# Light and heavy experts of a mixture taking turns step by step, with value products of attention on column tiles

## The chip, the cores and the metric

The kernel runs on one core of a Trainium2 chip. The core has a matrix engine (TensorE), a vector engine (VectorE), a scalar engine (ScalarE), GpSimd, and SyncE, which here issues the DMA transfers in program order ("SP" in the profile). Products are accumulated in eight PSUM banks of 128 partitions by 512 fp32 values. The metric is the time of one execution on the device in microseconds, the median of the runs.

## The reference, cut to what matters

The program is a stack of layers on 256 rows of 1024 values: retention, a feed-forward layer, dilated attention, a feed-forward layer, a layer that joins a convolution mixer and neighborhood attention, a feed-forward layer, a Fourier mixer, and a mixture of experts. All is fp32. The two attentions and the mixture are what the change touches:

```python
p = softmax(scores + bias)                    # per head and block of 128 queries
o = einsum('bhqk,bhkd->bhqd', p, v)           # head width 64 (dilated) or 32 (neighborhood)

logits = h @ w_router + b_router              # 8 experts
top_val, top_idx = lax.top_k(logits, 2)       # each row goes to 2 of them
out = zeros_like(h)
for e in range(8):
    out = out + gate[..., e:e+1] * ((silu(h @ w1[e]) * (h @ w3[e])) @ w2[e])   # 1024 -> 3584 -> 1024
```

## The kernel before, in words

**Mixture of experts.** The router's choices are counted per expert, and `order_experts` ranks the experts by their number of rows on VectorE (expert 0 is always rank 0; the count of the other ranks decides). Ranks 0 to 3 are "heavy" and handled on a tile of 128 rows, ranks 4 to 7 are "light" and handled on 64 rows. If an expert has more rows than its tile, a second pass at the end does the rest; it is skipped here at run time.

For each expert, `select` writes a 0/1 matrix P (Pz for a light one) from the row positions `posm`, and `gather` multiplies it with the rows: the expert's own rows, transposed, come out (`hgh`, `hgl` for a heavy one, `hx` for a light one). Then come seven steps `u`, each over 512 of the 3584 hidden columns. A step has two parts:

- `first` loads 512 columns of `w1` and of `w3`, 2 MB each, into wide slots (`rawx` and `rawy`, a ring of four), and multiplies. A heavy expert splits each fp32 weight into a high and a low part (`wh` by ScalarE at L113, `wl` by VectorE at L114) and does three products for each (L1067), on the whole 128x128 array. A light one takes the fp32 weights as they are, with 64 columns of rows standing, so that `w1` goes to the upper and `w3` to the lower column tile of the array in turn (L1055). ScalarE and VectorE then form silu times product (`tm`, L1163 and L1164).
- `turn` transposes this by TensorE (L1078) into `eTh`, `eTl` or `eTx`, and `back` multiplies it with two 1 MB units of `w2` (ring of `raw` and `x`), on the whole array (L1107) or on column tiles (L1095). In the program this second part of a step is written after the first products of the next step.

At step 6 `spread` transposes P, and `scatter` adds the result, weighted by the gate, to the rows (L1135, L1136). The plan runs one whole expert after another: heavy rank 0 with all its seven steps, light rank 4 with its seven, heavy rank 1, and so on. Loads are issued by SyncE in the order in which the program uses them, each when its slot is free. PSUM has four banks for products (`mm`), two for transposes (`tp`) and two for the rest (`aux`).

**Attention.** For one head and one block of 128 queries, the scores S are products in an `aux` bank. `attend` adds the bias with a running minimum (L388, VectorE), takes the exponential (L390, ScalarE), normalizes (L392, L393, VectorE), transposes by TensorE (L396) and copies to P (L398, ScalarE). Then four value products follow (L488 in the dilated attention, 64 columns wide; L932 in the neighborhood attention, 32 wide), each on the columns of the array that the head's number gives. The heads are written one after another.

The functions that the change touches:

Of the kernel before, what the change touches and what calls it, by code (L numbers as in the profile page):

```python
# [18 lines left out]
F32 = mybir.dt.float32  # L19
# [33 lines left out]
class Net:  # L53
    def __init__(s, tc, a, out, ctx):
# [10 lines left out]
        s.ps = s.pool("psum", 1, space=PSUM)  # L65
# [10 lines left out]

    def mm_tile(s, shape, name="mm"):
        return s.ps.tile(shape, F32, name=name, tag="mm", bufs=4)

    def tp_tile(s, shape, name="tp"):  # L80
        return s.ps.tile(shape, F32, name=name, tag="tp", bufs=2)

    def aux_tile(s, shape, name="aux"):
        return s.ps.tile(shape, F32, name=name, tag="aux", bufs=2)
# [296 lines left out]
    def attend(s, pool, S, bias):  # L381
# [15 lines left out]
        P = pool.tile([128, 4, 128], F32, name="P")  # L397
# [3 lines left out]
    def dilated(s, x, xt):  # L401
        nc = s.nc
        with ExitStack() as ctx:
# [24 lines left out]
            for qd in range(4):  # L428
# [47 lines left out]
                for h in range(4):  # L476
                    c, e = h // 2, h % 2
                    hs = slice(64 * h, 64 * h + 64)
                    for b in range(2):
                        order = [(0, 0), (1, 0), (2, 0), (0, 1)] if b == 0 else [(0, 0), (0, 1), (1, 1), (2, 1)]  # L480
                        S = s.aux_tile([128, 4, 128])
                        for n, (g, kb) in enumerate(order):
                            nc.tensor.matmul(out=S[:, n, :], lhsT=Q[g][:, c, e, b * 128:b * 128 + 128],
                                             rhs=K[g][:, c, kb * 128:kb * 128 + 128], start=True, stop=True)
                        P = s.attend(p, S.rearrange("p n c -> p (n c)"),
                                     bias[:, h, 1 - b:5 - b, :].rearrange("p n c -> p (n c)"))
                        for n, (g, kb) in enumerate(order):
                            nc.tensor.matmul(out=O[64 * e:64 * e + 64, c, b * 128:b * 128 + 128],  # L488
                                             lhsT=V[g][:, kb, hs], rhs=P[:, n, :], start=n == 0, stop=n == 3)
# [416 lines left out]
    def neighborhood(s, ctx, yt):  # L906
# [4 lines left out]
        for c in range(4):  # L911
            O = s.mm_tile([128, 256])
            for hh in range(4):
                h = 4 * c + hh
                bt = biases[h % 2]
                for r2 in range(2):
                    src = bass.AP(tensor=rpb.tensor, offset=rpb.offset + h * 1905 + (5 - r2) * 127,
                                  ap=[[1, 64], [127, 6], [1, 64]])
                    nc.sync.dma_start(out=bt[64 - 64 * r2:128 - 64 * r2, 4:10, :], in_=src)
                nc.vector.tensor_tensor(out=bt[:, 4:10, :], in0=bt[:, 4:10, :],  # L920
                                        in1=mask[:, None, :].to_broadcast([128, 6, 64]), op=ALU.add)
                ds = slice(32 * h, 32 * h + 32)
                for b in range(2):
                    S = s.aux_tile([128, 2, 256])
                    q = qps[c // 2][:, c % 2, hh, b * 128:b * 128 + 128]
                    nc.tensor.matmul(out=S[:, b, :], lhsT=q, rhs=kt[:, c, :], start=True, stop=True)
                    nc.tensor.matmul(out=S[:, 1 - b, :], lhsT=q, rhs=s.kc[:, c, :], start=True, stop=True)
                    P = s.attend(p, S.rearrange("p n c -> p (n c)"),
                                 (bt[:, 6:14, :] if b == 0 else bt[:, 0:8, :]).rearrange("p m c -> p (m c)"))
# [74 lines left out]
    def experts(s, pc, m, plan, ss):  # L1004
# [136 lines left out]
        def prepare(n):  # L1141
            r, light, base = plan[n]
            P = select(r, light, base)
            return P, gather(P, light)

        ready, last = prepare(0), None
        for n, (r, light, _) in enumerate(plan):
            P, x = ready
            for u in range(7):
                g = first(r, light, u, x)  # L1150
                pms = next(g)
                hid = turn(last[1], last[3]) if last else None
                if pms is None:
                    pms = next(g)
                if n + 1 < len(plan) and u == (3 if plan[n + 1][1] != light else 6):
                    ready = prepare(n + 1)
                if last:
                    s.second(back, spread, scatter, last, hid, None)
                if u == 0:
                    po = [s.mm_tile([128, 512]) for _ in range(1 if light else 2)]  # L1160
                rows = 64 if light else 128
                sg = s.np.tile([128, 512], F32, name="tm")
                nc.scalar.activation(out=sg[0:rows], in_=pms[0], func=AF.Silu)  # L1163
                nc.vector.tensor_tensor(out=sg[0:rows], in0=sg[0:rows], in1=pms[1], op=ALU.mult)  # L1164
                last = r, light, u, sg, po, P
# [34 lines left out]
    def order_experts(s, q, pk, m, pc, posm, gate, iota, tri8):  # L1200
# [3 lines left out]
        cn = q.tile([128, NE], F32, name="cn")  # L1204
        nc.vector.tensor_copy(cn, pc)
# [25 lines left out]
        ids = pk.tile([128, NE], I32, name="ids")  # L1231
        by_rank(idf, iota[:, 0:NE])
        nc.vector.tensor_scalar(out=ids, in0=idf, scalar1=-1.0, scalar2=None, op0=ALU.add)
        m.posm = pk.tile([128, 2, NE], F32, name="posr")
        m.gate = pk.tile([128, 2, NE], F32, name="gater")
        for t in range(2):
            by_rank(m.posm[:, t, :], posm[:, t, :])
            by_rank(m.gate[:, t, :], gate[:, t, :])
# [5 lines left out]
        cnt = pk.tile([128, 1], I32, name="cnt")  # L1244
        nc.vector.tensor_copy(cnt, cf)
        return ids, cnt

    def moe(s, x):
# [5 lines left out]
        with ExitStack() as ctx:  # L1254
# [15 lines left out]
            with ExitStack() as c2:  # L1270
# [50 lines left out]
                for t in range(2):  # L1321
# [12 lines left out]
                ids, cnt = s.order_experts(q, pk, m, pc, posm, gate, iota, tri8)  # L1334
            ss = pk.tile([128, 2, 2], F32, name="ss")
            _, regs = nc.values_load_multi_w_load_instructions(ids[0:1, 1:NE], engines=(mybir.EngineType.SP,),
                                                               min_val=0, max_val=NE - 1)
            m.ids = [0] + list(regs)
            heavy, light = list(range(NH)), list(range(NH, NE))
            plan = []  # L1340
            for i in range(max(len(heavy), len(light))):
                plan += [(r, False, 0) for r in heavy[i:i + 1]] + [(r, True, 0) for r in light[i:i + 1]]
            with ExitStack() as c2:
                s.experts(s.pool("moe_c", 1, c2), m, plan, ss)
# [245 lines left out]
```

## Time and profile before

| | us |
|---|---|
| median of three runs | 2341.37 (2340.36 to 2343.44) |
| the profiled execution | 2343.06 |
| its span, first to last instruction | 2341.2 |
| TensorE busy | 2244.8 (96% of the span) |
| VectorE busy | 1482.3 (63%) |
| ScalarE busy | 1079.1 (46%) |
| DMA, 639.74 MB | mean 273 GB/s |

The span is cut into instructions per engine, each with its start, its duration, its line of the kernel and the tiles it writes and reads (out<-in). Idle time before an instruction is put down to what ended it. A fp32 matmul can leave more than one record, and the recorded end of a matmul lies after the start of the next, since they are pipelined; so the distance of starts is the rate. TensorE's granted clock is given for a stretch as a share of full speed; its mean over the span is 0.980.

### The profile page before, as it was taken

How to read it: one execution, taken by the hardware profiler on the slowest of the kernel's cores; microseconds unless marked ns; L12 is line 12 of the kernel's file. 1: busy time of each engine (PE TensorE's matmuls, PEld its weight loads, DVE VectorE, ACT ScalarE, POOL GpSimd, SP SyncE). 2: the span in 40 equal slices, each digit the busy share in tenths (PEclk: the TensorE clock that was granted, in tenths of full speed). 3: DMA queues.
4: the chain of work that ended last, by engine and by line, in shares of the span. 5: the costliest groups of instructions: out<-in, count | busy, mean ns of one | idle time of the engine just before them, and what ended most of it. 6: DMA issues, size and time to landing. Idle time of an engine off the chain costs nothing. (4 is left out here: it accounts for less than half of the span.)

```text
span 2341.2 us, 34240 instructions
## 1 busy us (share of the span) xinstructions
PE 2244.8 (96%) x13729; PEld 1792.7 (77%) x13729; DVE 1482.3 (63%) x2018; ACT 1079.1 (46%) x1424; POOL 33.4 (1%) x39
## 2 busy tenths in 40 slices
PE   8999999999999999999899997999999999999996
PEld 8987988899998998987799786863685378447832
DVE  6987897867746555785665557850794179228821
ACT  4433543454444544655544445740673167126611
POOL 0000000000000000100000000000000000000000
PEclk9999999999999999999999997999999999999998
DMA  8676778777642554642365636889998999899986
GB/s 316 240 257 220 279 258 287 263 261 264 238 167 105 203 195 168 222 157 41 112 212 205 240 116 259 338 326 426 424 406 329 412 425 392 331 426 425 391 345 250
DMA packets 99710, 639.74 MB, mean 273 GB/s; under 512 B 22551, under 2 KB 33432, under 8 KB 39512
## 3 DMA queue, kind: packets, MB, share of 16 engines
q1 hardware_dynamic: 99128, 636.71, 71.1%
q8 instruction: 109, 1.79, 0.3%
q10 hardware_dynamic: 416, 0.78, 0.1%
q14 instruction: 57, 0.47, 0.1%
HBM read 634.17 MB, written 3.28 MB: 272 GB/s over the span
## 5 line engine op out<-in xcount | busy, mean ns | idle before, releaser
L113 ACT ACTIVATE wh<-raw 128x1024 fp32r<-128x1024 f32 x476 | 502.6, 1060 | 569.2 <-PE mm L154 263.2
L114 DVE TENSOR_TENSOR wl<-raw,wh 128x1024 fp32r<-128x1024 f32 x476 | 576.2, 1221 | 250.4 <-ACT wh L113 247.6
L154 PE MATMUL mm<-xTh,wh 128*128 128x256 f32 x1600 | 447.4, 280 | 0.7 <-ACT tm L816 0.7
L154 PE MATMUL mm<-xTh,wl 128*128 128x256 f32 x1600 | 446.0, 279 | 0.0
L154 PE MATMUL mm<-xTl,wh 128*128 128x256 f32 x1600 | 445.3, 278 | 0.0
L154 PEld LDWEIGHTS mm<-xTh,wh 128*128 128x128 f32 x1600 | 301.2, 188 | 7.5 <-issue 5.6
L154 PEld LDWEIGHTS mm<-xTh,wl 128*128 128x128 f32 x1600 | 300.8, 188 | 4.1 <-issue 4.1
L154 PEld LDWEIGHTS mm<-xTl,wh 128*128 128x128 f32 x1600 | 301.1, 188 | 3.5 <-issue 3.5
L1164 DVE TENSOR_TENSOR tm<-tm,mm 128x512 f32<-128x512 f32 (+1 forms) x56 | 38.0, 679 | 252.8 <-ACT tm L1163 252.8
L1067 PE MATMUL mm<-wh,hgh 128*128 128x512 f32 x448 | 179.9, 402 | 0.0
L1067 PE MATMUL mm<-wl,hgh 128*128 128x512 f32 x448 | 178.8, 399 | 0.0
L1067 PE MATMUL mm<-wh,hgl 128*128 128x512 f32 x448 | 177.5, 396 | 0.0
L170 PE MATMUL mm<-wh,xTh 128*128 128x256 f32 x608 | 173.8, 287 | 2.9 <-ACT wh L113 2.5
L170 PE MATMUL mm<-wh,xTl 128*128 128x256 f32 x608 | 174.1, 287 | 1.5 <-DVE xTl L144 1.5
L170 PE MATMUL mm<-wl,xTh 128*128 128x256 f32 x608 | 173.8, 286 | 0.6 <-DVE wl L114 0.5
L114 DVE TENSOR_TENSOR wl<-rawx,wh 128x1024 fp32r<-128x1024 f32 x128 | 150.7, 1220 | 16.1 <-ACT wh L113 15.0
L113 ACT ACTIVATE wh<-rawx 128x1024 fp32r<-128x1024 f32 x128 | 133.0, 1059 | 38.4 <-PE mm L1067 14.7
L1055 PE MATMUL mm<-rawy,hx 128*64 128x512 f32 x512 | 135.4, 637 | 14.2 <-DMA rawy<-in_moe_w_dram 14.2
L526 DVE CUSTOM_DVE_ANT_0 araw<-araw,cond 128x1024 f32<-128x1024 f32 x96 | 115.7, 1217 | 27.0 <-DMA araw<-in_w_ada_dram 26.9
L1163 ACT ACTIVATE tm<-mm 128x512 f32<-128x512 f32 (+1 forms) x56 | 33.0, 589 | 206.3 <-PE mm L1055 199.0
L170 PEld LDWEIGHTS mm<-wh,xTh 128*128 128x128 f32 x608 | 117.8, 194 | 5.3 <-ACT wh L113 2.9
L170 PEld LDWEIGHTS mm<-wh,xTl 128*128 128x128 f32 x608 | 118.5, 195 | 2.8 <-DVE xTl L144 2.3
(358 smaller groups left out, 3670.2 us busy)
## 6 DMA issues: line engine op xcount, KB each, us to landing
rawx<-in_moe_w_dram SPq DMA_DIRECT2D x56, 2048.0 KB, 9.7
rawy<-in_moe_w_dram SPq DMA_DIRECT2D x56, 2048.0 KB, 11.9
raw<-in_moe_w_dram SPq DMA_DIRECT2D x84, 1024.0 KB, 14.7
araw<-in_w_ada_dram SPq DMA_DIRECT2D x48, 1024.0 KB, 5.1
raw<-in_ffn_w_up_dram SPq DMA_DIRECT2D x44, 1024.0 KB, 4.8
raw<-in_attn_w_in_dram SPq DMA_DIRECT2D x36, 1024.0 KB, 5.0
raw<-in_ffn_w_dram SPq DMA_DIRECT2D x33, 1024.0 KB, 4.9
x<-in_moe_w_dram SPq DMA_DIRECT2D x28, 1024.0 KB, 12.2
```

The lines of the kernel that those rows point to most:

```text
L113: nc.scalar.activation(out=h, in_=v, func=AF.Copy)
L114: nc.vector.tensor_tensor(out=l, in0=v, in1=h.bitcast(F32), op=ALU.subtract)
L154: s.nc.tensor.matmul(out=p[:, j, :], lhsT=a[:, kc, :], rhs=b[:, kc, :], start=n == 0, stop=n == 23)
L170: s.nc.tensor.matmul(out=p[:, tb if to is None else to, :], lhsT=a[:, kc, tb, :], rhs=b[:, kc % 4, :], start=n == 0, stop=n == 23)
L526: nc.vector.tensor_tensor_reduce(out=out, in0=r[:, j, :], in1=cond[src], scale=1.0, scalar=0.0, op0=ALU.mult, op1=ALU.add, accum_out=dst)
L1055: nc.tensor.matmul(out=ps[half], lhsT=x[:, kc, :], rhs=w[:, kc, :], start=kc == 0, stop=kc == 7)
L1067: nc.tensor.matmul(out=pm, lhsT=a[:, kc, :], rhs=b[:, kc % 2, :], start=n == 0, stop=n == 23)
L1163: nc.scalar.activation(out=sg[0:rows], in_=pms[0], func=AF.Silu)
L1164: nc.vector.tensor_tensor(out=sg[0:rows], in0=sg[0:rows], in1=pms[1], op=ALU.mult)
```

## The change

- The plan is a list of single steps. It begins with two steps of the first heavy expert and then takes a light and a heavy step in turn, so that the four light experts (28 steps) run beside the four heavy ones (28 steps).
- While the experts run, PSUM has five banks for products, one for transposes and two for the rest.
- The ranking of the experts is written behind the first step of the first expert, whose rows are gathered ahead of it (rank 0 needs no ranking). The positions, gates and counts that this needs are copied to tiles of their own.
- In both attentions two heads go through the scores and `attend` together, and their value products are written in turn, one for each head, so that neighbours stand on different column tiles. P has four buffers.

The core of the diff:

```diff
+            s.banks(5, 1, 2)
...
-            heavy, light = list(range(NH)), list(range(NH, NE))
-            plan = []
-            for i in range(max(len(heavy), len(light))):
-                plan += [(r, False, 0) for r in heavy[i:i + 1]] + [(r, True, 0) for r in light[i:i + 1]]
+            heavy = [(r, False, 0, u) for r in range(NH) for u in range(7)]
+            light = [(r, True, 0, u) for r in range(NH, NE) for u in range(7)]
+
+            plan = heavy[:2]
+            for i in range(max(len(heavy) - 2, len(light))):
+                plan += light[i:i + 1] + heavy[i + 2:i + 3]
...
-        ready, last = prepare(0), None
-        for n, (r, light, _) in enumerate(plan):
-            P, x = ready
-            for u in range(7):
-                g = first(r, light, u, x)
+        ready, last, late = {}, None, None
+        prepare(*order[False].pop(0))
+        for n, (r, light, _, u) in enumerate(plan):
+            P, x, po = ready[r]
+            g = first(r, light, u, x)
+            pms = next(g)
+            hid = turn(last[1], last[3]) if last else None
+            if pms is None:
                 pms = next(g)
...
+            if n == 1 and rank:
+                rank()
+                if order[True]:
+                    late = True
+            if late is not None and order[late]:
+                prepare(*order[late].pop(0))
+            late = None
+            if u == 6 and order[light]:
+                if n + 1 < len(plan) and plan[n + 1][1] == light:
+                    prepare(*order[light].pop(0))
+                else:
+                    late = light
+            if last:
+                s.second(back, spread, scatter, last, hid, None)
...
                 for b in range(2):
...
+                    P = []
+                    for hh, bt in enumerate(biases, h0):
+                        S = s.aux_tile([128, 2, 256])
...
+                        P.append(s.attend(p, S.rearrange("p n c -> p (n c)"),
+                                          (bt[:, 6:14, :] if b == 0 else bt[:, 0:8, :]).rearrange("p m c -> p (m c)")))
                     vs = [vt, vt, s.vc, s.vc] if b == 0 else [s.vc, s.vc, vt, vt]
                     for n in range(4):
-                        nc.tensor.matmul(out=O[32 * hh:32 * hh + 32, b * 128:b * 128 + 128],
-                                         lhsT=vs[n][:, n % 2, ds], rhs=P[:, n, :], start=n == 0, stop=n == 3,
-                                         tile_position=(0, 32 * hh))
+                        for i, hh in enumerate((h0, h0 + 1)):
+                            nc.tensor.matmul(out=O[32 * hh:32 * hh + 32, b * 128:b * 128 + 128],
+                                             lhsT=vs[n][:, n % 2, 128 * c + 32 * hh:128 * c + 32 * hh + 32],
+                                             rhs=P[i][:, n, :], start=n == 0, stop=n == 3, tile_position=(0, 32 * hh))
```

TensorE, in the middle of a light expert before. L1055 are the first products, L1095 those with `w2`, L1078 the turns:

```order
L1095 MATMUL mm<-raw,eTx 64x512 x8
L1078 MATMUL tp<-ident,tm 128x64 x4
L1055 MATMUL mm<-rawx,hx 64x512 x16
L1095 MATMUL mm<-raw,eTx 64x512 x4
L1095 MATMUL mm<-x,eTx 64x512 x4
L1055 MATMUL mm<-rawy,hx 64x512
```

TensorE in the change, in the middle of the stage, where L1079 is the last product with `w3` of a heavy step, L1107 the light expert's `w2`, L1090 the heavy step's turn, L1067 the first products of the next light step and L1119 the heavy expert's `w2`:

```order
L1079 MATMUL mm<-wl,hgh 128x512
L1107 MATMUL mm<-raw,eTx 64x512 x8
L1090 MATMUL tp<-ident,tm 128x128 x4
L1067 MATMUL mm<-rawx,hx 64x512 x16
L1119 MATMUL mm<-wh,eTh 128x512 x2
L1119 MATMUL mm<-wh,eTl 128x512 x2
L1119 MATMUL mm<-wl,eTh 128x512 x2
```

The products of a light step, which stood in one row with those of the next light step, now stand in two groups of 8 and 16 among the heavy step's products on the whole array, and the light step's own turn stands between the heavy products too.

VectorE ahead of the first gather before: `hm` are the modulated rows, `mrl` their low part, `byr` the ranking's work tile, P the first selection matrix:

```order
L1284 TENSOR_TENSOR hm<-hm,brow 128x512
L1227 TENSOR_TENSOR byr<-iota,R 128x64
L1228 TENSOR_REDUCE idf<-byr 128x8
L1233 TENSOR_SCALAR ids<-idf 128x8
...
L1243 TENSOR_REDUCE cf<-cr 128x1
L1245 CAST cnt<-cf 128x1
L1023 TENSOR_SCALAR P<-iota,posr 128x128 x2
```

The same place on VectorE in the change:

```order
L1340 SCALAR_TENSOR_TENSOR posm<-aux,sel 128x16
L1365 COPY cn<-aux 128x8
L1363 COPY posr<-posm 128x2
L150 TENSOR_TENSOR mrl<-hm,mrh 128x512
L1035 TENSOR_SCALAR P<-iota,posr 128x128 x2
L1229 COPY key<-cn 128x8
```

P now stands ahead of the ranking, which begins with `key`.

## Rows read from the trace of the kernel before

**Rows 1.** 25 us windows: TensorE, weight loads, VectorE, ScalarE, GpSimd busy; granted clock; DMA share, GB/s.

```profile
1705.00:1730.00 25.00, 25.00 (x111) 20.30 (x111) 22.24 (x21) 20.32 (x23) 0.00 (x0) 1.00 1.01 422
...
1755.00:1780.00 25.00, 25.00 (x113) 16.90 (x113) 16.82 (x18) 13.89 (x16) 0.00 (x0) 1.00 0.72 285
...
1830.00:1855.00 25.00, 24.16 (x112) 8.33 (x109) 1.36 (x2) 2.26 (x5) 0.00 (x0) 1.00 1.02 429
...
1855.00:1880.00 25.00, 21.95 (x89) 11.46 (x90) 10.38 (x11) 9.84 (x13) 0.00 (x0) 0.86 1.01 426
...
1405.00:1430.00 25.00, 10.88 (x49) 10.53 (x49) 15.90 (x60) 4.36 (x8) 0.26 (x1) 0.50 0.61 243
```

**Rows 2.** TensorE's waits from 1400 us on: releaser, total us, times, longest.

```profile
PE mm L1055 <- DMA rawy<-in_moe_w_dram: 14.2, 5, 3.5
...
PE mm L1055 <- DMA rawx<-in_moe_w_dram: 4.6, 2, 3.4
```

**Rows 3.** TensorE's timeline, two turns in heavy steps: start, duration, instruction.

```profile
1721.08 0.60 PE L1078 MATMUL tp<-ident,tm 128*128 128x128 f32 x4
...
1738.26 0.60 PE L1078 MATMUL tp<-ident,tm 128*128 128x128 f32 x4
```

**Rows 4.** TensorE's timeline in a light expert: an undisturbed step, then one that waits.

```profile
1804.54 1.07 PE L1055 MATMUL mm<-rawy,hx 128*64 128x512 f32 x2
...
1805.54 0.44 PE L1036 MATMUL aux<-P,mrh 128*128 128x128 f32 x2
...
1808.69 6.65 PE L1055 MATMUL mm<-rawy,hx 128*64 128x512 f32 x29
...
1819.14 0.46 PE L1078 MATMUL tp<-ident,tm 64*128 64x64 f32 x4
...
1819.53 1.94 PE L1055 MATMUL mm<-rawx,hx 128*64 128x512 f32 x8
...
1854.14 0.46 PE L1078 MATMUL tp<-ident,tm 64*128 64x64 f32 x4
...
1858.05 9.25 PE L1055 MATMUL mm<-rawy,hx 128*64 128x512 f32 x29 [3.45 <-DMA rawy<-in_moe_w_dram]
...
1871.09 0.46 PE L1078 MATMUL tp<-ident,tm 64*128 64x64 f32 x4
```

**Rows 5.** The page's DMA issues of expert weights: count, size, us to landing.

```profile
rawx<-in_moe_w_dram SPq DMA_DIRECT2D x56, 2048.0 KB, 9.7
...
rawy<-in_moe_w_dram SPq DMA_DIRECT2D x56, 2048.0 KB, 11.9
...
raw<-in_moe_w_dram SPq DMA_DIRECT2D x84, 1024.0 KB, 14.7
...
x<-in_moe_w_dram SPq DMA_DIRECT2D x28, 1024.0 KB, 12.2
```

**Rows 6.** SyncE's DMA queue, first wide loads of two heavy experts.

```profile
1648.74 5.40 SPq L104 DMA_DIRECT2D rawx<-in_moe_w_dram  x2
...
1873.99 5.40 SPq L104 DMA_DIRECT2D rawx<-in_moe_w_dram  x2
```

**Rows 7.** VectorE's timeline ahead of the first selection matrix.

```profile
1413.13 1.89 DVE L1284 TENSOR_TENSOR hm<-hm,brow 128x512 f32<-128x512 f32 x3
...
1417.34 0.22 DVE L1227 TENSOR_TENSOR byr<-iota,R 128x64 f32<-128x64 f32 x1
...
1421.61 0.48 DVE L1023 TENSOR_SCALAR P<-iota,posr 128x128 fp32r<-128x128 f32 x2
```

**Rows 8.** The same window view, of the neighborhood attention.

```profile
1046.00:1131.00 85.00, 82.33 (x533) 63.18 (x532) 50.38 (x151) 46.37 (x103) 0.00 (x0) 1.00 0.22 50
```

**Rows 9.** Groups of instructions in that stage: busy us, mean ns, idle before.

```profile
L932 PE MATMUL mm<-P,vc 128*32 128x128 f32 x128 | 19.4, 275 | 0.3 <-ACT P L398 0.3
...
L398 ACT ACTIVATE P<-tp 128x512 f32<-128x512 f32 x32 | 18.6, 593 | 22.2 <-PE tp L396 22.2
```

**Rows 10.** TensorE's timeline there, four records of value products.

```profile
1072.32 0.62 PE L932 MATMUL mm<-P,nv 128*32 128x128 f32 x4 [0.31 <-ACT P L398]
```

More of the change, by code (lines that the diff above doesn't have):

```diff
@@ L64, in __init__ @@
         s.dp = s.pool("scratch", 1, space=DRAM)
[L65 removed]
+        s.psx = ctx.enter_context(ExitStack())
+        s.banks(4, 2, 2)
         s.ident = s.con.tile([128, 128], F32, name="ident")
@@ new lines, in neighborhood @@
+            for h0 in range(0, 4, 2):
+                for hh, bt in enumerate(biases, h0):
+                    for r2 in range(2):
+                        src = bass.AP(tensor=rpb.tensor, offset=rpb.offset + (4 * c + hh) * 1905 + (5 - r2) * 127,
+                                      ap=[[1, 64], [127, 6], [1, 64]])
+                        nc.sync.dma_start(out=bt[64 - 64 * r2:128 - 64 * r2, 4:10, :], in_=src)
+                    nc.vector.tensor_tensor(out=bt[:, 4:10, :], in0=bt[:, 4:10, :],
+                                            in1=mask[:, None, :].to_broadcast([128, 6, 64]), op=ALU.add)
+                for b in range(2):
+                    P = []
+                    for hh, bt in enumerate(biases, h0):
+                        S = s.aux_tile([128, 2, 256])
+                        q = qps[c // 2][:, c % 2, hh, b * 128:b * 128 + 128]
+                        nc.tensor.matmul(out=S[:, b, :], lhsT=q, rhs=kt[:, c, :], start=True, stop=True)
+                        nc.tensor.matmul(out=S[:, 1 - b, :], lhsT=q, rhs=s.kc[:, c, :], start=True, stop=True)
+                        P.append(s.attend(p, S.rearrange("p n c -> p (n c)"),
+                                          (bt[:, 6:14, :] if b == 0 else bt[:, 0:8, :]).rearrange("p m c -> p (m c)")))
@@ L1002, in fourier, with experts @@
             return s.gated_residual(x, po, grow, then)
-    def experts(s, pc, m, plan, ss):
+    def experts(s, pc, m, plan, ss, rank=None):
         nc = s.nc
@@ L1139, in scatter, with prepare @@
                         s.squares(m.acc[:, t, :], c, ss[:, t, :], s.tp_tile([128, 512]))
-        def prepare(n):
-            r, light, base = plan[n]
+        def prepare(r, light, base):
             P = select(r, light, base)
-            return P, gather(P, light)
-        ready, last = prepare(0), None
-        for n, (r, light, _) in enumerate(plan):
-            P, x = ready
-            for u in range(7):
-                g = first(r, light, u, x)
-                pms = next(g)
[L1152 to L1165, printed above, removed]
@@ new lines, in prepare @@
+            ready[r] = P, gather(P, light), []
+        order = {k: [x[:3] for x in plan if x[1] == k and x[3] == 0] for k in (False, True)}
+        ready, last, late = {}, None, None
[6 more added lines that the diff above has]
+            if pms is None:
+                pms = next(g)
+            if n == 1 and rank:
[12 more added lines that the diff above has]
+                s.second(back, spread, scatter, last, hid, None)
+            if u == 0:
+                po.extend(s.mm_tile([128, 512]) for _ in range(1 if light else 2))
+            rows = 64 if light else 128
+            sg = s.np.tile([128, 512], F32, name="tm")
+            nc.scalar.activation(out=sg[0:rows], in_=pms[0], func=AF.Silu)
+            nc.vector.tensor_tensor(out=sg[0:rows], in0=sg[0:rows], in1=pms[1], op=ALU.mult)
+            last = r, light, u, sg, po, P
@@ L1230, in order_experts @@
         idf = q.tile([128, NE], F32, name="idf")
-        ids = pk.tile([128, NE], I32, name="ids")
         by_rank(idf, iota[:, 0:NE])
-        nc.vector.tensor_scalar(out=ids, in0=idf, scalar1=-1.0, scalar2=None, op0=ALU.add)
-        m.posm = pk.tile([128, 2, NE], F32, name="posr")
-        m.gate = pk.tile([128, 2, NE], F32, name="gater")
+        nc.vector.tensor_scalar(out=m.idt, in0=idf, scalar1=-1.0, scalar2=None, op0=ALU.add)
+        _, regs = nc.values_load_multi_w_load_instructions(m.idt[0:1, 1:NE], engines=(mybir.EngineType.SP,), min_val=0,
+                                                           max_val=NE - 1)
+        m.ids += list(regs)
         for t in range(2):
-            by_rank(m.posm[:, t, :], posm[:, t, :])
-            by_rank(m.gate[:, t, :], gate[:, t, :])
+            for out, v in ((m.posm, posm), (m.gate, gate)):
+                r = q.tile([128, NE], F32, name="byr1")
+                by_rank(r, v[:, t, :])
+                nc.vector.tensor_copy(out[:, t, 1:NE], r[:, 1:NE])
         cr = q.tile([128, NE], F32, name="cr")
```

79 lines of the change are left out of this document (35 added, 44 removed).

## The prediction

> **What bounds the kernel now.** I read the chain of waits of TensorE over the expert stage first, then 25 us windows of one pair of experts, then the issues of the weight loads, then TensorE's own timeline inside one step of each kind.
>
> The expert stage takes 40% of the time (it starts near 1400 us of 2341.2), and TensorE is nearly always busy there. But it is busy with different limits. While a heavy expert runs, TensorE, VectorE (22.2 of 25 us) and the DMA engines (share 1.01) are all full [rows 1]. The row at the end of the heavy expert shows the DMA share fall to 0.72 and the rate to 285 GB/s: the slots are full, and TensorE sets the pace. While the light expert runs, VectorE does 1.4 of 25 us, and the DMA share climbs back to 1.02 at 429 GB/s; in the next window TensorE's granted clock is 0.86 [rows 1]. So the light half drains the weight buffers and at its end waits for a transfer. The waits say the same: TensorE waited 14.2 us for `rawy` and 4.6 us for `rawx`, 18.8 us in all [rows 2].
>
> Two periods give the sizes. One heavy step lasts 1738.26 - 1721.08 = 17.2 us between two turns [rows 3]. One undisturbed light step takes 1819.14 - 1808.69 = 10.45 us plus the 0.39 us to the next step's first matmul, so 10.84 us; the step whose load came late takes 1871.09 - 1854.14 = 16.95 us, with a wait of 3.45 us inside it [rows 4]. Of the 6.1 us too much, 3.45 are the wait and the other 2.66 follow it: 29 matmuls take 9.25 us behind the wait where they took 6.65, and the granted clock is lower there. Each microsecond waited costs 6.11 / 3.45 = 1.77 us.
>
> Demand against supply: the loads of the eight experts are 56 + 56 of 2 MB and 84 + 28 of 1 MB [rows 5], 336 MB (binary), 352.3 million bytes, 88.1 for one heavy and one light expert. At 426 GB/s that is 206.8 us. The first wide load of a heavy expert is issued at 1648.74 and of the next at 1873.99, so a pair takes 225.3 us [rows 6]. There are 18.5 us per pair, 74 in four, between the pace of today and the pace of the DMA alone. That is the most that any order of the steps could give.
>
> **Part by part: taking turns.** The steps stay the same, so TensorE's work stays, 17.2 + 10.84 = 28.0 us for one heavy and one light step. The loads of two such steps are 12.58 million bytes, 29.5 us at 426 GB/s. Inside a stretch of plain steps the DMA would thus fall behind by 1.5 us per two steps, 10 us in seven; gathers and scatters, in which nothing is consumed, give it back (225.3 minus all 8.3 us of wait and lowered clock, which I work out next, is 217, and 217 is more than 206.8). A transfer lands 9.7 to 14.7 us after its issue in this stage [rows 5], so the slots hold about that backlog. I therefore let nearly all waits for weights go: 18.8 us times 1.77 is 33.3 us, or 8.3 per pair. I leave 2 us of them in. Bounds: nothing gained (the waits only move), and 74 us (DMA alone is the limit).
>
> **More changes between whole array and column tiles.** In the order before, light steps stand in a row and TensorE stays on its two column tiles, except for the turns. In the order of the change, one light step's second half and the next one's first half are two separate islands among full-array matmuls, and the 64-row turn stands between full-array matmuls too: one more island per light step, 27 in all. What an island costs has rows on both sides. Leaving the tiles for a turn and coming back shows nothing: turn at 1819.14, tiles again at 1819.53, which is what four transposes take [rows 4]. A lone pair of tile matmuls between gather matmuls takes 1805.54 - 1804.54 = 1.00 us, where a pair in a stream takes 0.43 (28 spacings of 29 matmuls in 6.65 - 0.59 us, 0.216 each): 0.57 too much [rows 4]. I take the middle, 0.28 us, because the islands are 8 and 16 matmuls long and only their edges are bare: 27 x 0.28 = 7.7 us lost; bounds 0 and 15.4.
>
> **Ranking behind the first gather.** TensorE stands idle until the first selection matrix P is there, at a granted clock of 0.50 in that window [rows 1]. VectorE writes P at 1421.61; from 1417.34 on it has done small ranking operations, and a single large one of 0.69 us [rows 7]. 4.27 - 0.69 = 3.6 us go, and another 0.9 us of ranking that stood ahead of the modulation at 1413.13 (some ten small operations, partly beside waits). I count 4.5 us; bounds 3 and 6. The register load of the expert numbers now stands in SP's queue ahead of the second expert's loads, but the slots are full at this time (243 GB/s in the window) [rows 1], so nothing is lost there. The ranking itself now lies on VectorE beside the first heavy step's splits, some 4 us late for one step, while its loads wait for free slots anyway.
>
> **Five product banks, one for turns.** Two experts in flight need three banks for their sums, and two are left for products, as before in a heavy expert. One bank for turns makes a turn wait for the copy of the one before; turns are 10 us apart, so I count nothing, and 0.5 us at the tail, where four squares share the bank. It would cost more only if spread and turn of two experts fell together, about 1 us at each of eight ends.
>
> **Attention.** The neighborhood stage is 85 us with TensorE busy 82.3, VectorE 50.4 and ScalarE 46.4 [rows 8]. Its value products are 32 columns wide and one after another. A set of scores (one head, one block of queries) has four, and the trace two records for each, 256 for the 32 sets, half of them in the row shown [rows 9]. Four records take 0.62 us, and one 0.275, so they follow each other by 0.115 us [rows 9, 10] and a set takes 0.92. On two column tiles in turn two heads should run at once, as the halves of a light expert do, so half of that, 0.46 us per set and 14.7 us in all, is the most. The dilated stage has as many sets (4 groups of heads, 4 heads, 2 blocks), on 64 columns: 14.7 us again by the same spacing. Against this stands the chain of a set: ScalarE already waits 22.2 us for the transposed scores [rows 9], and both heads of a pair must now be ready before the first product. Bounds 0 and 29.4; I take 11, somewhat under the middle, since TensorE is the fullest of the three by far.
>
> **The sum.** -33.3 + 2 + 7.7 - 4.5 + 0.5 - 11 = -38.6 us. The profiled execution took 2343.06 us (1.7 above the median of the runs, 2341.37), so 2304.5 in its terms and 2302.8 in the median's. I say 2303.
>
> **Rivals.** (a) Islands cost a drain at either edge. A tile matmul lasts 0.59 us and the stream moves by 0.216, so emptying the array costs up to 0.37 us, twice per island: 27 x 0.75 = 20 us in place of 7.7, and 2315. For it: the lone pair. Against it: the turn at 1819.14. The Trainium skill has it as a rule ("TensorEngine Tiling (Array Packing)", section "Key Properties"): a change of tiling mode, not of the tile alone, drains TensorE. The rows here agree for the lone pair and not for the turn. Chance 0.15. (b) The attention chain is bound by its latency, and pairs gain nothing: 2314. For it ScalarE's 22.2 us, against it TensorE's 82.3 of 85. Chance 0.12. (c) The DMA is the bound all through: the backlog of 1.5 us per two steps grows past what the slots hold and half of the wait comes back, 17 us: 2320. Chance 0.07. (d) Slower: in the mixed order, the light step's silu product queues on VectorE and ScalarE behind the splits of a heavy weight that has not landed, and TensorE waits for both. It decides from the point at which a pair of steps loses 38.6 / 27 = 1.4 us more; at 2 us it is 2357. For it: the engines work strictly in order and a split waits for its transfer. Against it: they would be loaded 16 of 28 us where it is now 22.2 of 25. Chance 0.07. (e) The turn-taking does nothing since loads wait in one SP queue in the same order as they are used, and starved steps only move: about 2330 with attention and start. Chance 0.05. The forecast has 0.54.
>
> **Range and chances.** (a), (b) and (c) lie inside 2280 to 2325; the low end is attention at its full 29.4 (18 less) with islands nearly free (4 to 5 less). Outside are (d), most of (e) and a little of the rest at either end. A difference under 0.2% (4.7 us) can hardly be told from none here. Faster: the forecast, (a) to (c) and (e) but for a few hundredths, 0.90. Same 0.03, slower 0.07.
>
> **What would show it.** Right: TensorE's waits for `rawx` and `rawy` under 3 us in all; no window of the stage under clock 0.95; a period of 215 to 219 us for 14 steps; DMA share nearly even over the stage, 0.93 to 1.0; the first gather at 1417; the neighborhood stage 6 us shorter. Wrong: gaps of 0.3 us or more at each end of the column-tile matmuls (a); ScalarE waits in attention as long as the saving (b); rows of DMA waits spread over heavy and light matmuls (c); waits of TensorE for `tm`, `wh` or `wl` (d). The forecast fails altogether if the slots are handed out in an order in which a light load that is not needed yet holds the place of a heavy one that is.

## The result, and the profile after

| | before | changed |
|---|---|---|
| median of four runs, us | 2342.4 (2340.36 to 2344.18) | 2315.03 (2311.44 to 2317.26) |
| profiled execution, us | 2343.06 | 2317.26 |
| its span, us | 2341.2 | 2315.2 |

The changed kernel is faster: the ratio to the kernel before is 0.9883, with a 95% interval from 0.9871 to 0.9895, so 27.4 us by the medians. The prediction was 2303, 38.6 us less than the 2341.37 it started from.

The waits of TensorE from 1380 us to the end, in the changed kernel (engine, tile and line that waited, what ended the wait, total, times, longest):

```profile
PE aux L1338 <- DVE sel L1336: 7.0, 1, 7.0
PE mm L1079 <- DVE wl L120: 4.1, 3, 1.4
PE aux L1147 <- ACT n L149: 4.0, 5, 1.5
```

No wait for `rawx` or `rawy` is left; there were 18.8 us of them [rows 2]. The windows of 25 us (columns as in [rows 1]) show what took their place:

```profile
1765.00:1790.00 25.00, 25.00 (x113) 16.00 (x111) 15.93 (x15) 13.06 (x15) 0.00 (x0) 1.00 1.01 426
1890.00:1915.00 25.00, 23.90 (x105) 13.25 (x102) 17.61 (x19) 12.82 (x15) 0.00 (x0) 0.98 0.69 265
1665.00:1690.00 25.00, 23.90 (x102) 11.81 (x102) 15.29 (x17) 11.20 (x15) 0.00 (x0) 0.93 0.70 269
```

In the stretch of plain steps the DMA engines are full and TensorE works all the time. At the end of each pair of experts the rate falls to between 265 and 304, because all slots are full: from 1880 to 1920 us SyncE's queue waits 35 us for TensorE and VectorE to be done with a slot. The slots hold the backlog, as the prediction had it, and VectorE is far from full (15.9 us of 25, where heavy steps in a row had 22.2). The clock is not even: the third window has 0.93.

The timeline of TensorE shows one step pair (start, duration, instruction):

```profile
1975.05 0.46 PE L1090 MATMUL tp<-ident,tm 64*128 64x64 f32 x4
1975.44 0.50 PE L1079 MATMUL mm<-wh,hgh 128*128 128x512 f32 x1
...
1981.24 3.65 PE L1107 MATMUL mm<-raw,eTx 128*64 128x512 f32 x16
1984.82 0.66 PE L1090 MATMUL tp<-ident,tm 128*128 128x128 f32 x4
1985.41 7.09 PE L1067 MATMUL mm<-rawx,hx 128*64 128x512 f32 x32
1992.42 0.74 PE L1119 MATMUL mm<-wh,eTh 128*128 128x512 f32 x2
...
2013.60 0.66 PE L1090 MATMUL tp<-ident,tm 128*128 128x128 f32 x4
```

From the heavy turn at 1984.82 to the next heavy one at 2013.60 there are 28.78 us, and nothing in them waits for data. What did the same work take before? The heavy step took 17.18 us [rows 3]. For the light step the prediction has 10.84 [rows 4], but these hold only 46 of a step's 48 records, since two had run ahead of the gather. The next two light steps of the kernel before are undisturbed too:

```profile
1819.53 7.09 PE L1055 MATMUL mm<-rawx,hx 128*64 128x512 f32 x32
1826.44 1.89 PE L1095 MATMUL mm<-raw,eTx 128*64 128x512 f32 x8
1828.16 1.89 PE L1095 MATMUL mm<-x,eTx 128*64 128x512 f32 x8
1829.88 1.02 PE L1055 MATMUL mm<-rawy,hx 128*64 128x512 f32 x2
1830.83 0.46 PE L1078 MATMUL tp<-ident,tm 64*128 64x64 f32 x4
...
1841.72 0.46 PE L1078 MATMUL tp<-ident,tm 64*128 64x64 f32 x4
```

From the turn at 1819.14 to the one at 1830.83 there are 50 records in 11.69 us, and to the next turn 48 in 10.89. Two records take 0.43, so 96 records take 22.15 us and a light step 11.08. The pair of before thus took 28.26 us, and that of the change takes 0.52 more: 14.0 us if all 27 pairs were plain ones (an estimate). The places: the heavy turn holds 0.59 us between two islands (0.36 before, from 1721.08 to the next product at 1721.44), the 24 products from 1975.44 to 1981.24 take 5.80 us (5.58 among their like), and the two islands of 16 and 32 records take 3.58 and 7.01, where as many spacings of 0.216 are 3.46 and 6.91. Together this is more than 0.52, because the light steps of before were not free of loss either: 48 spacings and a turn are 10.8 us, and they took 11.08.

### The profile page after: what moved, and what is told of

Read it like the earlier page. It is cut to its first block, busy times and chain, and to the rows that moved or that the text cites. A ratio compares the mean times of both kernels' runs of the same rounds, so it can differ in the third digit from the quotient of the medians.

```text
span 2315.2 us, 34156 instructions
## 1 busy us (share of the span) xinstructions
PE 2236.4 (97%) x13729; PEld 1766.7 (76%) x13729; DVE 1486.4 (64%) x2024; ACT 1072.7 (46%) x1424; POOL 33.5 (1%) x39
## 5 line engine op out<-in xcount | busy, mean ns | idle before, releaser
L119 ACT ACTIVATE wh<-raw 128x1024 fp32r<-128x1024 f32 x446 | 468.8, 1059 | 552.1 <-PE mm L160 256.8
L120 DVE TENSOR_TENSOR wl<-raw,wh 128x1024 fp32r<-128x1024 f32 x446 | 538.9, 1220 | 246.4 <-ACT wh L119 245.4
L120 DVE TENSOR_TENSOR wl<-rawy,wh 128x1024 fp32r<-128x1024 f32 x216 | 255.6, 1222 | 87.1 <-ACT wh L119 86.5
L119 ACT ACTIVATE wh<-rawy 128x1024 fp32r<-128x1024 f32 x216 | 224.1, 1057 | 52.3 <-PE mm L1079 27.9
L1067 PE MATMUL mm<-rawx,hx 128*64 128x512 f32 x864 | 202.7, 595 | 0.0
L1079 PE MATMUL mm<-wl,hgh 128*128 128x512 f32 x448 | 179.6, 402 | 4.1 <-DVE wl L120 4.1
L1079 PE MATMUL mm<-wh,hgh 128*128 128x512 f32 x448 | 181.1, 404 | 0.0
L1079 PE MATMUL mm<-wh,hgl 128*128 128x512 f32 x448 | 177.8, 397 | 0.0
L1067 PEld LDWEIGHTS mm<-rawx,hx 128*64 128x64 f32 x864 | 62.3, 137 | 117.8 <-issue 117.3
L535 DVE CUSTOM_DVE_ANT_0 araw<-araw,cond 128x1024 f32<-128x1024 f32 x96 | 115.7, 1218 | 33.3 <-DMA araw<-in_w_ada_dram 33.2
L176 PEld LDWEIGHTS mm<-wl,xTh 128*128 128x128 f32 x608 | 118.4, 195 | 1.5 <-DVE wl L120 1.0
```

Source lines behind the costliest of these rows:

```text
L119: nc.scalar.activation(out=h, in_=v, func=AF.Copy)
L120: nc.vector.tensor_tensor(out=l, in0=v, in1=h.bitcast(F32), op=ALU.subtract)
L176: s.nc.tensor.matmul(out=p[:, tb if to is None else to, :], lhsT=a[:, kc, tb, :], rhs=b[:, kc % 4, :], start=n == 0, stop=n == 23)
L535: nc.vector.tensor_tensor_reduce(out=out, in0=r[:, j, :], in1=cond[src], scale=1.0, scalar=0.0, op0=ALU.mult, op1=ALU.add, accum_out=dst)
L1067: nc.tensor.matmul(out=ps[half], lhsT=x[:, kc, :], rhs=w[:, kc, :], start=kc == 0, stop=kc == 7)
L1079: nc.tensor.matmul(out=pm, lhsT=a[:, kc, :], rhs=b[:, kc % 2, :], start=n == 0, stop=n == 23)
```

## The experiments

All are set against the kernel before on the same chip, whose median lay from 2339.92 to 2342.4 us in the batches. Differences to the changed kernel go across batches, so one or two us of them mean little.

**Attention alone.** The kernel before with the attention parts of the diff.

> The kernel before with the two attentions of the change alone (experts as before). Theory of the prediction: 11 us less, from both attentions. Theory read from the trace of the change, in which the router begins 6.9 us earlier, the neighborhood stage keeps its length (83.5 and 83.8 us from the first score to the last value product) and the dilated one begins 1.7 us later and ends 6.3 us earlier: 7 to 8 us less, all from the dilated attention, so 2334 to 2336. Rival: a part of the 6.9 us comes from elsewhere, then 2338 or more.

2330.61 us, ratio 0.9958 (0.9943 to 0.9973): 9.9 us. The groups of the dilated stage (480 to 720 us) show where it comes from:

```profile
L484 PE MATMUL aux<-k,qp 128*128 128x128 f32 x256 | 35.8, 281 | 2.6 <-DVE nm L388 2.6
...
L491 PE MATMUL mm<-P,v 128*64 128x128 f32 x256 | 24.3, 282 | 0.5
```

The scores are as before, and the value products are busy 24.3 us; the same group had 32.5 in the kernel before. The stage, from its first score to its last value product, falls from 237.4 to 229.4 us. In the neighborhood stage the same measure goes from 83.5 to 83.0. So the gain is near the forecast's 11, and what the stages show of it (8.5 us) comes nearly all from one of the two.

**The kernel before's order of steps, all else as changed.**

```diff
-            plan = heavy[:2]
-            for i in range(max(len(heavy) - 2, len(light))):
-                plan += light[i:i + 1] + heavy[i + 2:i + 3]
+            plan = []
+            for i in range(0, 28, 7):
+                plan += heavy[i:i + 7] + light[i:i + 7]
```

> The changed kernel with the plan of the kernel before (seven steps of a heavy expert, then seven of a light one); ranking behind the first gather, banks and attention stay. Theory: the turns themselves are worth 13 us (the first product of the experts to the end is 912.2 us before and 899.3 after), attention 7 and ranking 6, so this run is 13 us above the changed kernel, about 2329, and has the waits for rawx and rawy back, 15 us or more. Rival: the turns are worth nothing after the cost of the column tile edges, and all the gain is attention and the start: 2316.

2334.67 us, ratio 0.998 (0.9969 to 0.999), 19.6 us above the changed kernel. Its waits of TensorE for weights are back:

```profile
PE mm L1067 <- DMA rawx<-in_moe_w_dram: 13.8, 4, 3.4
PE mm L1067 <- DMA rawy<-in_moe_w_dram: 11.4, 6, 2.4
```

So taking turns is what took them away. Its net worth is 13.8 us by the spans of the profiled executions and 19.6 by the medians; the profiled one lies at the low end of this run's range (2331.08 of 2331.08 to 2342.96).

**Two and three steps in turn.**

```diff
+            for i in range(0, max(len(heavy) - 2, len(light)), 2):
+                plan += light[i:i + 2] + heavy[i + 2:i + 4]
```

> The changed kernel with two light steps and two heavy steps in turn. In the written order this has 112 passages between whole-array and column-tile or 64-row work on TensorE, against 156 with single steps and 28 one expert after another. A step pair takes 28.78 us in the changed kernel and 28.0 by the steps before; 0.77 x 27 = 21 us over 126 passages more is 0.165 us each. Theory (the passages cost): 44 x 0.165 = 7 us less than the changed kernel, 2308. Rival (heavy steps are slower beside light ones whatever the passages, by shared memory or engines): as the changed kernel, 2315. Rival (DMA): two light steps on end bring waits for rawx and rawy back, 2318 or more.

> Three light steps and three heavy steps in turn: 80 passages. Theory: 76 x 0.165 = 12.5 us less than the changed kernel, 2302.5, with no waits for weights, since three light steps use 12 us more of transfer than they last and the slots hold two steps of each kind. Rival (DMA): waits of 4 us and more return at the end of each block, 2315 or more. Rival (passages are free): 2315.

2363.74 us (ratio 1.01, 1.0083 to 1.0118) and 2349.81 us (1.0041, 1.0026 to 1.0055): slower than the kernel before, which none of the theories had said. No wait for a transfer of weights stands among the larger ones. The timeline of TensorE with two steps in turn:

```profile
1755.04 0.66 PE L1090 MATMUL tp<-ident,tm 128*128 128x128 f32 x4
...
1775.04 0.27 PE L1090 MATMUL tp<-ident,tm 128*128 128x128 f32 x1
...
1776.24 0.55 PE L1090 MATMUL tp<-ident,tm 128*128 128x128 f32 x3
...
1816.73 0.66 PE L1090 MATMUL tp<-ident,tm 128*128 128x128 f32 x4
1819.02 0.50 PE L1079 MATMUL mm<-wh,hgh 128*128 128x512 f32 x1 [1.63 <-ACT wh L119]
```

and that of ScalarE at the same time:

```profile
1817.42 0.60 ACT L149 ACTIVATE eTh<-tp 128x512 fp32r<-128x512 f32 x1 [9.18 <-PE tp L1090]
1817.92 3.89 ACT L119 ACTIVATE wh<-rawy 128x1024 fp32r<-128x1024 f32 x4
```

ScalarE stood idle for 9.18 us until the heavy turn was done, copied it, and only then split the next heavy step's weights, because the splits stand behind the copy in its order. TensorE waits for the first of them. Four steps (turn at 1755.04 to turn at 1816.73) take 61.69 us, where two pairs of the changed kernel take 57.56. Of these 4.13 us, 2.2 are waits for the splits (1.63 for `wh`, 0.54 for `wl`). Part of the rest is the order of the products: at 1775.04 a heavy turn is broken up by two records of light products and takes 1.2 us to its second transpose. Over the whole run the waits for `wh` and `wl` ahead of the first products are 21.0 us with two steps in turn and 18.5 with three, where the changed kernel has 4.1: between a third and a half of what these runs lose against it (48.7 and 34.8). This is the mechanism of the slower rival, (d), in another place: an engine that works in order, with a split queued behind something that comes late. The rest was not taken apart, and whether fewer passages save time these two runs can't tell.

**The light turn on the whole array.**

```diff
-            pt = s.tp_tile([128, 4, rows])
+            pt = s.tp_tile([128, 4, 128])
...
-                nc.tensor.transpose(pt[:, k, :], sg[0:rows, k * 128:k * 128 + 128], s.ident[0:rows, 0:rows])
+                nc.tensor.transpose(pt[:, k, :], sg[:, k * 128:k * 128 + 128], s.ident)
...
+            if light:
+                nc.gpsimd.memset(sg[64:128], 0.0)
```

> The changed kernel with the light turn on the whole array: GpSimd clears the lower 64 rows of the light product, and TensorE transposes 128 rows of it (64 columns of the result are used). Nothing else is moved. In the changed kernel the 24 products ahead of the light turn take 5.69 us and the 24 behind it 5.80, where 24 products among their like took 5.58. Theory (a passage of TensorE to another row or column size costs): 0.3 us less for each of 27 turns, 8 us less than the changed kernel, 2307. Rival (heavy products are slower beside a light expert for another reason): the 5.69 and 5.80 stay, 2315.

2305.54 us, ratio 0.9845 (0.9826 to 0.9863), 9.5 us below the changed kernel. The pairs, by the heavy turns on TensorE (the light turn is the one between):

```profile
1974.80 0.66 PE L1089 MATMUL tp<-ident,tm 128*128 128x128 f32 x4
...
1993.71 0.60 PE L1089 MATMUL tp<-ident,tm 128*128 128x128 f32 x4
...
2003.42 0.66 PE L1089 MATMUL tp<-ident,tm 128*128 128x128 f32 x4
```

28.62 us per pair, 0.16 less, 4.3 us in all. That is half of what was expected of the passages. Another 4.9 us of the two profiled executions come from three places at the ends of experts where the changed kernel ran at the lower clock level (17.44, 23.08 and 23.08 us between two turns, where its undisturbed likes take 15.96, 21.38 and 21.38) and this one did not, one of them below (TensorE's timeline, 16 records of light products behind a gather of light rows, in the changed kernel and then here):

```profile
1665.74 5.35 PE L1107 MATMUL mm<-raw,eTx 128*64 128x512 f32 x16
```

```profile
1660.43 3.65 PE L1106 MATMUL mm<-raw,eTx 128*64 128x512 f32 x16
```

The granted clock is 0.93 from 1665 to 1690 us in the changed kernel and 1.00 from 1650 to 1700 here. Why it falls in one of them is not settled; the work ahead of it is the same but for the light turn. The turn does not forbid it: the two runs below that keep this turn, on the same experts, have one such place (0.93 from 1650 to 1675 us) and two (0.93 from 1640 to 1665 and from 2080 to 2105). So these 4.9 us may be a matter of the execution, and only the 4.3 are shown to be the turn's.

**One island per pair.** The loop is written anew so that the light expert's first products and the `w2` products of its previous step stand together, and heavy `w2` products come behind the next heavy step's `w1` products; the heavy turn is held behind the island by an order edge. In the second version the light turn is held behind the `w1` products too.

```diff
+            if hl and isl[0]:
+                with s.tc.issue_after(isl[0].ins):
+                    hid = turn(False, hl[3])
...
+            if ll and ll[1] is None:
+                with s.tc.issue_after(isl[1].ins):
+                    ll = ll[0], turn(True, ll[0][3])
```

> As turn_full, and the order of a step pair is changed so that the light expert's first products and the w2 products of its previous step stand next to each other with no turn between: first products of the next light step, w2 of the light step before, heavy turn, w1 products of the next heavy step, light turn, w2 products of the heavy step, w3 products of the next heavy step. Two passages per pair instead of six. Theory: 28.78 us per pair fall to 28.2, 15 us less than the changed kernel, about 2300, with the light products of a pair in one stretch of 10.5 us. Rival (splits, seen with blocks of two and three): the heavy weights' splits stand behind the turn's copy on ScalarE, TensorE waits for wh some 1.5 us per pair, and the run is 2340 or more. Rival (DMA): at 28.2 us per pair the transfers, 29.5 us, are the bound, waits for weights return between the gathers, and half is gained, 2307.

> merged, with the light turn held behind the w1 products of the next heavy step. In merged eight turns stood directly behind a heavy turn, and waited 1.5 us each for its copy, since there is one bank for turns; the plain step pairs took 28.28 us as expected. Theory (2 passages per pair in place of turn_full's 4, at 0.15 us, and no wait for the bank): 0.34 us less per pair than turn_full, 9 us, 2297; step pairs of 28.3 us and no turn that waits for eTl. Rival (the two scatters and the gathers, which stand nearer together in this order, lose it again): 2306 or more, with waits of TensorE for n, Pz or eTh at the ends of the experts.

2330.53 us (0.9953, 0.9936 to 0.997) and 2337.81 us (0.9981, 0.9972 to 0.999): both lose against the changed kernel, and 25.0 and 32.3 us against the run with the light turn on the whole array, on which they stand. But the plain pairs do what was expected. TensorE's timeline of the first version, heavy turn, light turn, heavy turn:

```profile
1969.22 0.66 PE L1091 MATMUL tp<-ident,tm 128*128 128x128 f32 x4
1975.32 0.60 PE L1091 MATMUL tp<-ident,tm 128*128 128x128 f32 x4
...
1997.50 0.66 PE L1091 MATMUL tp<-ident,tm 128*128 128x128 f32 x4
```

28.28 us per pair. The loss lies at the ends of the experts. In the first version a light turn stands right behind a heavy one eight times and waits for the one turn bank, in the second the bank is free, and the split stands behind the turn's copy again (waits of TensorE):

```profile
PE tp L1091 <- DVE eTl L150: 12.0, 8, 1.5
```

```profile
PE mm L1081 <- ACT wh L119: 13.7, 10, 1.6
PE mm L1081 <- DVE wl L120: 12.5, 17, 1.1
```

**Half of the neighborhood's value products.** The kernel before, `for n in (0, 3)` in place of four.

> The kernel before, with two of the four value products of each set left out in the neighborhood attention (the output is not the reference's). TensorE has 0.46 us less per set, 14.7 us in all, as much as a perfect run of two at a time would give, and the chain of a set keeps all its steps but has no second head to wait for. Theory of the prediction (TensorE is the fullest and sets the pace): the stage shortens by 10 us or more, 2331 or less. Rival (the chain through VectorE, ScalarE and TensorE sets it): the 83.5 us stay within 4 us, 2337 or more.

The routing of the rows changes with the values, so that the second pass over the experts runs and the whole takes 3356 us; only the stage can be read. Its value products, last at 1116.0 (the first score is at 1046.8):

```profile
L932 PE MATMUL mm<-P,nv x64: 272/273/297, 1053.7 to 1116.0; 128*32 128x128 f32 x64
```

69.2 us in place of 83.5, 14.3 of the 14.7 that TensorE has less. TensorE sets the pace there, and the chain of a single head doesn't. So the pairing has the gain within reach and gives it back.

**The order inside a pair.** In the changed kernel the first product of the ready head goes ahead and seven wait. Both runs stand on the light turn on the whole array. In the first the head that is ready last begins, in both attentions (the neighborhood's lines below); in the second the products of a pair of the neighborhood attention are also written behind the scores of the next pair.

```diff
-                        for i, hh in enumerate((h0, h0 + 1)):
+                        for i, hh in ((1, h0 + 1), (0, h0)):
```

> turn_full, and in both attentions the value products begin with the head whose weights are ready last. In the changed kernel the order on TensorE puts one value product of the first head ahead of other work and the rest behind it (1 and 7), and TensorE waits for the second head's P in between; here eight stand together. Theory (the pairing in the neighborhood stage gained nothing because two heads wait for each other, while TensorE sets the pace of that stage, as the run with half the products showed: 69.2 us for 83.5): the stage falls from 82 to 76 us and the time from 2305.5 to about 2299. Rival: the wait stays, since P of the second head comes when it comes; 2305.

> As nb_rev, and in the neighborhood attention the value products of a pair are written behind the scores of the next pair, so that the chain of a pair has the next pair's work beside it. On TensorE they then stand in blocks of 16 products. Theory: the wait for P goes; four sets need 3.4 us of scores, 1.8 of transposes and 2 of products, 1.8 us per set, so the stage falls from 82 to 65 us at best, 70 with some waits, and the time from 2305.5 to about 2293. Rival (ScalarE and VectorE, 47 and 52 us busy in this stage, set the pace with their chain): not under 78 us, 2301.

2299.73 us (0.9816, 0.9799 to 0.9832) and 2296.59 us (0.9809, 0.9791 to 0.9828). The neighborhood stage takes 79.6 and 76.0 us from first score to last product, where the run that they stand on takes 82.1. The dilated stage falls as well, from 229.5 to 227.1 and 224.6, so about half of the gain is there. What the neighborhood's value products waited for, with PE and its weight loads together, in the changed kernel and then in the second run:

```profile
  ACT P L404: 16.7, 33
```

```profile
  issue: 1.3, 8
  ACT P L404: 0.4, 1
```

In the kernel before it was 7.9 us, so the pairing itself had doubled the wait for P. This wait was the missing gain. With it gone the stage stops at 76.0 and not at 70; the scores then wait for VectorE to free their banks (3.5 us on their matmuls, by the groups of that stage), and the rest was not followed. These are the fastest kernels of the study, and the two can't be told from each other.

**Ranking ahead again, and attention as before.** In the first, the early copies of rank 0's positions are left out and the ranking is written ahead of the gather; the second is the changed kernel with the old attention code.

> The changed kernel with the ranking ahead of the first selection matrix again (the ranked positions of rank 0 are no longer copied early); turns, banks and attention stay. Theory of the prediction: 4.5 us more than the changed kernel, 2319.5. By the traces of before and of the change (23.9 and 17.5 us from the router's first product to the first gather): 6 us more, 2321, with 22 us or more from router to gather. Rival (the start is hidden, since the weights are loaded meanwhile and the experts' stage ends when the transfers end): no more than 1 us, 2316.

> The changed kernel with the two attentions of the kernel before. Theory (the parts add up): 9.9 us more than the changed kernel, as the attentions alone took off the kernel before, so 2325; 237 us in the dilated stage in place of 229. Rival (the parts overlap, since later stages take up what was gained): 2318 or less.

2322.11 us (0.9919, 0.9905 to 0.9932), 7.1 above the changed kernel, and 2324.18 us (0.9926, 0.9913 to 0.994), 9.2 above it. The first gather waits for the ranking again:

```profile
1409.40 0.45 PE L1048 MATMUL aux<-P,mrh 128*128 128x128 f32 x1 [4.53 <-DVE byr L1250]
```

The attention adds to the rest what it gives alone. For the ranking the profiled execution, the lowest of its five, shows less than the medians: 21.2 us from the router's first product to the first gather, where the changed kernel has 17.6, so 3.7 us.

## Why the prediction was right, and where it was not

**The mechanism held.** The light half of a pair drained the slots, the waits for weights and the lowered clock behind them were the price, and taking turns removed them; the run with the old order has the waits back, 25.2 us. By the turns in TensorE's timeline, the seven light steps of before that waited for weights took 30.0 us more than undisturbed ones with as many records, 11.08 us for 48 and 10.84 for 46 (6.1, 1.3, 6.1, 1.4, 6.1, 3.7 and 5.2). The prediction had 33.3, since it gave all waits the factor 1.77 of one step; over the seven it is 1.59. It left 2 us in, and the changed kernel still has 4.9 at the lower clock. From the first gather to the end the stage went from 919.0 to 906.2 us, 12.8 less. The parts, -30.0 + 4.9 + 14.0 for the step pairs, give 11.1; the other 1.7 are not placed.

**The term that was mis-sized: passages between whole array and column tiles.** The step was "I take the middle, 0.28 us [...] 27 x 0.28 = 7.7 us lost; bounds 0 and 15.4." The pairs grew by 0.52 us, 14.0 in all: nearly twice the forecast, close to the upper bound. Three things failed. The count was of islands, one more per light step, but a plain pair has six passages (into and out of two islands, and into and out of the 64-row turn). The price was read at a turn between tile products, where a passage shows nothing because it hides behind what the row calls "four transposes". And the 28.0 us to compare with held a light step that was two records short. Three kernels with the same products and 6, 4 and 2 passages take 28.78, 28.62 and 28.28 us a pair. The first difference gives 0.08 us for each passage of the light turn, the second 0.17 for each edge of an island; the second is an estimate, because that order also takes the heavy turn out from between two islands. The Trainium skill's rule ("TensorEngine Tiling (Array Packing)", section "Key Properties", a change of tiling mode drains TensorE) agrees with these rows in that the passages cost; a drain by itself no row shows.

**Rival (a).** Its time, 2315, is what was measured, but by luck. It priced an edge at 0.37 us, about twice the 0.17, and came to 20 us where the pairs grew by 14.0; this error of 6 us is made up by the waits and the clock, which gave back 25.1 us and not 31.3.

**Attention.** 11 us forecast, 9.2 to 9.9 measured. The size was right by chance: the dilated stage gave 8.0 and the neighborhood stage nothing. The reason given for a half, that both heads of a pair must be ready, is what the last runs show; the rival's reason, a stage bound by the chain's latency, falls with the run of half the products.

**Ranking.** 4.5 us forecast, bounds 3 and 6. The 23.8 us from the router's first product to the first gather became 17.6, so 6.2 less; undoing the step costs 3.7 by the trace and 7.1 by the medians. The change of order also brought the modulation forward, which the prediction did not count.

**Banks.** No wait for a product bank shows in the changed kernel, and two waits for the turn bank, 0.9 us in all, beside the 0.5 of the forecast; the single turn bank bites when two turns meet, as in the first order with one island (12.0 us).

**DMA (rival c)** did not come: step pairs of 28.8 us are so near the 29.5 us of transfer that the backlog fits the slots. **Slower (rival d)** did not come in the changed kernel, whose only waits for `wl` are three of 1.4 us, but its mechanism is between a third and a half of the loss with two and three steps in turn, and most of it in the second order with one island (29.3 us of waits for `wh` and `wl`). The prediction's argument against it, that VectorE is loaded less, was no argument: the engine was idle when the split was late.

**The sum.** Forecast -33.3 + 2 + 7.7 - 4.5 + 0.5 - 11 = -38.6. Measured part by part, -30.0 + 4.9 + 14.0 - 6.2 - 9.5 = -26.8, beside 27.4 by the medians and 25.8 by the profiled executions. So the forecast went 11 us too far: 6.3 by the passages and 6.2 by the waits and the clock, while the errors of the smaller terms nearly cancel.

**Its signs.** No wait for `rawx` or `rawy` is left, as forecast. The first gather came at 1409 us and not at 1417, since the attention ended earlier too. The others failed: two windows have a clock of 0.93, 14 steps take 221 to 223 us and not 215 to 219, the DMA share falls to 0.7 at the ends of the experts, and the neighborhood stage is not 6 us shorter (83.8 us where it was 83.5).

## What to carry to other kernels

Interleaving a stage that is short of transfers with one that is short of TensorE takes the waits away when the slots hold the backlog between; count every change of the tile's size that the new order makes, turns included, and price them with two orders of the same work, after counting that the steps compared have as many records. What decides between orders is often the in-order queue of an idle engine: look where the next step's split stands relative to the copy that comes late. When two producers feed one run of alternating products, begin with the one that is ready last, so that the run does not start and stop.

## What was not expected of the hardware

- Between 128x128 matmuls and column-tile or 64-row ones the same work took 28.78, 28.62 and 28.28 us with 6, 4 and 2 passages: 0.08 us for a passage of the 64-row turn and, as an estimate, 0.17 for an edge of an island.
- Sixteen records of light products behind the same gather took 5.35 us at the lower clock in one kernel and 3.65 in another. Of three kernels with the light turn on the whole array and the same experts, one had no such place, one had one and one had two.
